# The causal mask of attention, added on VectorE together with the row minimum instead of as products on TensorE

## Chip, cores and metric

The kernel runs on one core of a Trainium2 chip. The metric is the device time of one execution in microseconds, the median of several runs. TensorE multiplies matrices into PSUM; VectorE and ScalarE read PSUM and SBUF and write SBUF here; GpSimd and SyncE mostly start transfers.

## The reference

Two decoder layers over 512 tokens of 1024 channels, in float32: a feed-forward part, a mixer, a second feed-forward part, each followed by a layer norm. The change lies in the mixer's attention. All of its units have this form (shortened):

```
def one_block(args):
    qs, qn, qp = args
    s = (jnp.einsum('bqhd,bkhd->bhqk', qn, k_nope, ...)
         + jnp.einsum('bqhd,bkd->bhqk', qp, k_pe, ...)) * scale
    s = jnp.where(kpos[None, :] <= qpos[:, None], s, NEG)     # causal mask
    p = jax.nn.softmax(s, axis=-1)
    return jnp.einsum('bhqk,bkhd->bqhd', p, v)
```

A layer has 8 heads of latent attention (MLA), and 8 heads of sparse attention (NSA) with two such branches each, over selected blocks and over a window; at this length both branches see all keys up to the query, and so have the same causal mask. A third branch works on 31 compressed keys with a mask of its own (`cmask`).

## The kernel before

Every float32 product is made of two or three products of a high and a low part (`float32r`). Weights come in chunks of 128 rows by up to 1024 columns, in the order of their use: SyncE loads `raw` (ring of 3), ScalarE copies the high part and VectorE subtracts to get the low part (`Stream.pump`, lines 272 and 201, ring `hl` of 4).

A mixer has 24 units of attention a layer: units 0 to 7 are MLA's, with three score passes (`kTh` with `qTh`, `kTl` with `qTh`, `kTh` with `qTl`, 96 rows), 8 to 23 are NSA's, with two passes of 128 rows that hold both parts. A unit (class `Unit`) has four steps. `scores` computes the scores of the four query blocks of 128 (`qb`), each against keys 0 to `(qb + 1) * 128`, so with 128, 256, 384 and 512 columns, into three PSUM banks `sc0` to `sc2`. After a block's passes, line 487 adds one more product into its last 128 columns: identity (`idb`) times mask (`maskb`, 0 or -1e30, both bf16). Line 492 takes the negated row maximum on VectorE (`nm`), and line 493 writes `P = exp(s + nm)` on ScalarE, with the row sum. `normalise` multiplies `P` by the reciprocal of the sum on VectorE (line 503). `transpose` transposes `P` on TensorE into three banks `pt` (line 511), which ScalarE copies to `ph` (line 517) and VectorE subtracts to `pl` (line 201). `pv` multiplies `ph` and `pl` with the values (lines 526 and 527), with the same column counts as the scores: 512, 384, 256, 128.

The order of these steps, and of projections and gate tiles (`gf`) between them, is written out by hand in `SCHEDULE` (S scores, N normalisation, T transposes, P product with values). Within it a scheduler sets each engine's queue; queues run in order. PSUM has eight banks, `P`, `ph` and `pl` come from 55 slabs of 512 columns.

Of the kernel before, what the change touches and what calls it, by code (L numbers as in the profile page):

```python
# [9 lines left out]
F32 = mybir.dt.float32  # L10
F32R = mybir.dt.float32r
BF16 = mybir.dt.bfloat16
AF = mybir.ActivationFunctionType
ALU = mybir.AluOpType
# [3 lines left out]
T = 512  # L18
# [8 lines left out]
NEG = -1e30  # L27

# columns of w_in in the order the kernel projects them
# [7 lines left out]
NSLAB = 55                # [128, 512] tiles for everything that lives for a while  # L37
RAW_RING = 3              # chunks of weights as loaded
HI_RING = 4               # chunks of weights in two parts
LOOK = 2                  # chunks split ahead of their use  # L40
LOOK_TAIL = 5             # the same for the chunks of a tail
LOOK_HEAD = 4             # and right after one
PIECE, PIECES = 256, 1    # the first chunks come in pieces of so many columns
PEND_AT = 3               # head tile before which the pending token blocks are transposed
TAIL = {NF: 5, KB: 4}     # last chunks of a down projection, used token block by token block
PASS, STAY, TAIL_KIND = 0, 1, 2

# The order in which the mixer's attention and what runs beside it is issued. Units of attention 0..23
# (8 heads of MLA, then 2 groups x 4 heads x 2 branches of NSA): Q queries, S scores, N normalisation,
# T transposed probabilities, P product with the values; K keys and G output of a pair of heads. "v" value  # L50
# projections, "m"/"n" halves of gate tiles, "pl"/"p" projection of MLA; "ql".."w" operands of a group,
# "c" compression.
# [62 lines left out]
def layer_plan(l):  # L115
    """Chunks of weights of one layer in the order of their use, each with whether it passes through the
    rings or stays in slabs; a chunk is a list of (matrix, layer, row block, first column, last column)."""
    p = []

    def add(c, kind=PASS):  # L120
        p.append((c, kind))

    def down(name, nkb):
        n = nkb // 2
        for dh in range(2):
            for i in range(n):
                add(down_chunk(name, l, dh, i), TAIL_KIND if dh == 1 and i >= n - TAIL[nkb] else PASS)

    def ffn(n):
        for fi in range(NF):  # L130
            add(stat_chunk(n + "_wg", l, fi * 128))
            add(stat_chunk(n + "_wu", l, fi * 128))
        down(n + "_wd", NF)

    def tok(c0, c1):
        for c in tok_chunks(l, c0, c1):
            add(c)

    ffn("ffn1")
    for m in range(4):  # L140
        add(gate_chunk(l, "m", m))
    tok(COL_A, COL_B)
    tok(COL_B, COL_C)
    add(uq_chunk(l, 0))
    add(uq_chunk(l, 1))
    add(ukv_chunk(l, 0), STAY)
    add(ukv_chunk(l, 1))
    for n in SCHEDULE:
        if n == "keys":
            tok(COL_C, COL_D)  # L150
        elif n == "v0":
            tok(COL_D, COL_GM)
        elif n[0] in "mn" and n[-1] == "a":
            add(gate_chunk(l, n[0], int(n[1])))
        elif n[:2] == "cw":
            add(w1_chunk(l, int(n[2]), int(n[3])))
        elif n == "c2":
            add(w2_chunk(l))
        elif n[0] == "p" and n[1] in "0246":
            add(proj_chunk(l, "w_proj_mla", int(n[1])))  # L160
    for m in range(0, KB, 2):
        add(proj_chunk(l, "w_proj_nsa", m))
    down("w_out", KB)
    ffn("ffn2")
    return p
# [11 lines left out]
def hybrid_kernel(ctx: ExitStack, tc: tile.TileContext, x, wflat, lnp, rmsg, small, cst, out):  # L177
# [40 lines left out]
    class Stream:  # L218
        """Weights in the order of their use: loaded ahead, then split into two float32r parts."""
# [72 lines left out]
    ct = const.tile([128, NCST - 128], F32, name="ct")  # L292

    def cs(name):
        o, n = CST[name]
        return ct[:, o - 128:o - 128 + n]
# [5 lines left out]
    maskb = const.tile([128, 128], BF16, name="maskb")  # L302
# [25 lines left out]
    def head_tiles(chunks, name):  # L328
        """The first weight tiles of a stage, on the tokens in the order in which they come."""
        chs = [W.get(c) for c in chunks]  # L330
        bs = [bank(f"{name}{i}") for i in range(len(chs))]
        for i, (b, ch) in enumerate(zip(bs, chs)):
            if i >= PEND_AT:
                while pend:
                    pend.pop(0)()
            stat_mms(b, ch, 0, 256, range(KB), True, True)
        for b, ch in zip(bs, chs):
            stat_mms(b, ch, 256, 512, range(KB), True, True)
            W.done()
        return bs  # L340

# [28 lines left out]
    def down(lhs, nkb, wname, l, c, eps, ln_idx, last):  # L370
        """xt <- LN(c * x + lhs^T @ w) for every token block; then x^T for the next stage."""
# [94 lines left out]
    class Unit:  # L466
        """One softmax: passes yields (lhsT, rhs) pairs of [K, T] tiles; v(kb) gives the values' two parts
        side by side, so that one product takes both: their shares come out in the two halves of the rows."""
# [6 lines left out]
        def scores(self):  # L475
            ps = [bank(f"sc{i}") for i in range(3)]
            self.P = [slab(f"P{i}") for i in range(3)]
            pp = self.passes()
            self.nm = work.tile([128, TB], F32, tag="nm", bufs=4, name="nm")
            self.l = work.tile([128, TB], F32, tag="l", bufs=4, name="l")  # L480
            for b, qbs in enumerate(BANKS):
                for qb in qbs:
                    off = SC[qb][1]
                    n = (qb + 1) * 128
                    for i, (a, k) in enumerate(pp):
                        mm(ps[b][:, off:off + n], a[:, qb * 128:(qb + 1) * 128], k[:, 0:n], start=i == 0, stop=False)  # L486
                    mm(ps[b][:, off + n - 128:off + n], idb, maskb, start=False, stop=True)  # L487
                for qb in qbs:
                    off = SC[qb][1]
                    n = (qb + 1) * 128  # L490
                    o = ps[b][:, off:off + n]
                    nc.vector.tensor_reduce(out=self.nm[:, qb:qb + 1], in_=o, axis=AX.X, op=ALU.max, negate=True)  # L492
                    act(out=self.P[b][:, off:off + n], in_=o, func=AF.Exp, bias=self.nm[:, qb:qb + 1], scale=1.0,  # L493
                        accum_out=self.l[:, qb:qb + 1])
# [37 lines left out]
    def mixer(l):  # L532
# [42 lines left out]
        # latents of the queries and of the keys and values, with the shared rotary key  # L575
# [24 lines left out]
        def latents():  # L600
# [8 lines left out]
            # below the keys of a head goes the shared rotary key  # L609
# [9 lines left out]
        # NSA queries  # L619
        bb = tok_all(COL_B, COL_C, "pb", latents)  # L620
        for tb in range(TB):
            t = slab(f"nq{tb}")
            act(out=t, in_=bb[tb], func=AF.Copy, scale=0.125)
# [4 lines left out]
        # MLA queries, keys and values  # L628
        scale = float(np.float32(96 ** -0.5))
# [30 lines left out]
        # NSA keys  # L660
# [13 lines left out]
        def halves(b, oc, odd):  # L674
            """Of a head's output the share of the values' high parts, and that of the low parts."""
# [24 lines left out]
        def proj_mla(m):  # L700
            """MLA's share of the gated sum, kept in place of its gates."""
# [20 lines left out]
        def mla_keys(j):  # L722
            """Keys of a pair of heads, in place of those of the pair before."""
# [51 lines left out]
        # gate tiles, in halves  # L775
# [19 lines left out]
        # NSA values and gates  # L795
# [25 lines left out]
        # compressed keys and values  # L821
# [19 lines left out]
        def c_blk(kind):  # L841
            """Rows (token parity, channel), columns (token pair of a window, group, window); the last column
            of a group holds the position embedding, so that the first layer gives its share there."""
# [29 lines left out]
        def c_w1(kind, jh):  # L873
            """Rows: windows, with the blocks' high parts, then with their low ones; columns: the same of the weights."""
# [24 lines left out]
        def c_gelu():  # L899
# [6 lines left out]
            # hidden units of the keys, and those of the values once per head of a group  # L906
# [39 lines left out]
        def group(g):  # L946
# [72 lines left out]
            def c_scores():  # L1019
# [14 lines left out]
                nc.vector.tensor_reduce(out=nm, in_=bv, axis=AX.X, op=ALU.max)  # L1034
                tt(out=pv, in0=bv, in1=nm.to_broadcast([128, 16, 32]), op=ALU.subtract)
                act(out=p, in_=p, func=AF.Exp)
# [71 lines left out]
        # gated sum of the two projections, transposed  # L1108
# [36 lines left out]
    with tc.manual_schedule(engines={mybir.EngineType.Pool}):  # L1145
# [22 lines left out]
        nc.vector.tensor_copy(out=maskb, in_=cs("mask"))  # L1168
# [8 lines left out]
def _constants():  # L1177
# [8 lines left out]
    put("mask", np.where(i[None, :] <= i[:, None], 0.0, NEG))  # L1186
    t = (np.arange(TB)[None, :] * 128 + i[:, None])
    cc = np.arange(32)
    put("cmask", np.where((16 * cc + 31)[None, None, :] <= np.maximum(t, 31)[:, :, None], 0.0, NEG))
# [13 lines left out]
    put("qcc", a * 96 ** -0.5)  # L1203
    put("qss", b * 96 ** -0.5)
# [55 lines left out]
```

## Time and profile before

| | |
|---|---|
| Median of 3 runs | 2288.7 us (2287.52 to 2290.64) |
| Span of the profiled execution | 2289.8 us |
| TensorE busy, of the span | 2274.2 us, 99% |
| VectorE busy | 1181.3 us, 52% |
| ScalarE busy | 859.7 us, 38% |
| Products of line 487 (mask) | 192 |
| Reductions of line 492, Exps of line 493 | 192 each |

The trace is of one execution; it gives a span and no time of its own beside it. TensorE's durations run from a product's start to its modelled end, and products overlap, so the time that a product takes of the engine is read from one start to the next. The attention of layer 1 lies at 468 to 708 us, that of layer 2 at 1602 to 1844 us.

### The profile page before, as it was taken

The page shows a single profiled execution, that of the slowest core. Times are in us where ns is not written, and L with a number is a line of the kernel's source. Part 1 is how long each engine was busy: PE and PEld are TensorE (multiplying, and loading weights), DVE is VectorE, ACT ScalarE, POOL GpSimd, SP SyncE. Part 2 cuts the span into 40 slices and gives each one's busy share as a digit, 9 for nine tenths or more (in the row PEclk, how much of TensorE's full clock was granted, in tenths as well). Part 3 has the DMA queues.
Part 4 walks back from the last instruction along what each step waited for, and adds up shares of the span by engine and source line. Part 5 has one row for each costly group of instructions (what it writes and reads, how often), then busy time and mean ns, then how long its engine had stood idle before and what let it go on. Part 6 is the DMA issues. An engine that isn't in the chain of part 4 may idle for free.

```text
span 2289.8 us, 29329 instructions
## 1 busy us (share of the span) xinstructions
PE 2274.2 (99%) x11590; PEld 1937.3 (85%) x11590; DVE 1181.3 (52%) x2039; ACT 859.7 (38%) x1618; POOL 103.0 (4%) x166
## 2 busy tenths in 40 slices
PE   9999999999999999999999999999999999999998
PEld 8888889998888888888898888899888889888886
DVE  4343335568877644443543433445787866343334
ACT  3222222469764232322222222224786642232220
POOL 0000001010001000000000000010100010000000
PEclk9999999999999999999999999999999999999999
DMA  5323333343225232233323233433432262323331
GB/s 170 102 92 101 107 115 109 121 136 124 93 84 191 99 111 94 100 102 105 115 74 101 92 101 106 139 107 107 126 127 88 70 232 81 102 92 101 106 106 65
DMA packets 86329, 251.57 MB, mean 110 GB/s; under 512 B 18224, under 2 KB 21424, under 8 KB 86192
## 3 DMA queue, kind: packets, MB, share of 16 engines
q1 hardware_dynamic: 75568, 215.09, 28.8%
q0 software_dynamic: 10624, 34.61, 4.3%
q8 instruction: 91, 1.49, 0.3%
q14 instruction: 46, 0.38, 0.1%
HBM read 225.55 MB, written 24.12 MB: 109 GB/s over the span
## 4 chain that ended last, share of the span: by engine, by line
PE 98%; ACT 1%; DMA 1%; DVE 0%; SPq 0%; issue 0%; DVEq 0%; ACTq 0%
PE gu L206 13%; PE gu L205 13%; PE gu L204 13%; PE d L206 8%; PE d L204 8%; PE d L205 8%; PE sc L486 3%; PE pt L511 2%; PE gf L204 2%; PE gf L206 2%; PE gf L205 2%; PE ffh L204 1%; PE ffh L206 1%; PE ffh L205 1%; PE on L527 1%; PE xtp L315 1%
## 5 line engine op out<-in xcount | busy, mean ns | idle before, releaser
L272 ACT ACTIVATE hl<-raw 128x1024 fp32r<-128x1024 f32 (+3 forms) x351 | 361.3, 1031 | 729.5 <-issue 341.8
L201 DVE TENSOR_TENSOR hl<-raw,hl 128x1024 fp32r<-128x1024 f32 (+3 forms) x351 | 416.8, 1189 | 397.7 <-ACT hl L272 397.3
L204 PE MATMUL gu<-xTh,hl 128*128 128x512 f32 x1280 | 498.0, 389 | 0.0
L205 PE MATMUL gu<-xTl,hl 128*128 128x512 f32 x1280 | 498.0, 389 | 0.0
L206 PE MATMUL gu<-xTh,hl 128*128 128x512 f32 x1280 | 497.9, 389 | 0.0
L205 PEld LDWEIGHTS gu<-xTl,hl 128*128 128x128 f32 x1280 | 240.3, 188 | 49.8
L206 PEld LDWEIGHTS gu<-xTh,hl 128*128 128x128 f32 x1280 | 240.3, 188 | 49.8
L204 PEld LDWEIGHTS gu<-xTh,hl 128*128 128x128 f32 x1280 | 240.3, 188 | 49.7
L204 PE MATMUL d<-hl,hh 128*128 128x512 f32 x544 | 211.6, 389 | 0.0
L205 PE MATMUL d<-hl,hh 128*128 128x512 f32 x544 | 211.6, 389 | 0.0
L206 PE MATMUL d<-hl,hl 128*128 128x512 f32 x544 | 211.6, 389 | 0.0
L427 DVE SCALAR_TENSOR_TENSOR t<-t,gu 128x512 f32<-128x512 f32 x80 | 55.0, 688 | 247.7 <-ACT t L426 247.7
L428 DVE TENSOR_TENSOR t<-t,gu 128x512 f32<-128x512 f32 x80 | 55.0, 688 | 210.8 <-PE gu L206 210.8
L426 ACT ACTIVATE t<-gu 128x512 f32<-128x512 f32 x80 | 47.9, 599 | 304.3 <-PE gu L206 304.3
L206 PEld LDWEIGHTS d<-hl,hl 128*128 128x128 f32 x544 | 102.1, 188 | 21.2
L205 PEld LDWEIGHTS d<-hl,hh 128*128 128x128 f32 x544 | 102.1, 188 | 21.2
L204 PEld LDWEIGHTS d<-hl,hh 128*128 128x128 f32 x544 | 102.1, 188 | 21.2
L493 ACT ACTIVATE P<-sc,nm 128x384 f32<-128x384 f32 x192 | 99.5, 527 | 40.6 <-DVE nm L492 32.4
L362 POOL TENSOR_TENSOR rs<-rs,ct 128x1 f32<-128x1 f32 x24 | 22.3, 930 | 1562.3 <-DVE rs L361 1562.3
L201 DVE TENSOR_TENSOR pl<-pt,ph 128x512 fp32r<-128x512 f32 x144 | 78.9, 596 | 24.8 <-ACT ph L517 24.6
L492 DVE TENSOR_REDUCE nm<-sc 128x1 f32<-128x384 f32 x192 | 84.3, 486 | 14.0 <-PE sc L487 11.4
L318 ACT ACTIVATE xTh<-xtp 128x512 fp32r<-128x512 f32 x48 | 26.2, 596 | 157.7 <-PE xtp L315 157.7
(310 smaller groups left out, 3951.3 us busy)
## 6 DMA issues: line engine op xcount, KB each, us to landing
raw<-in_wflat_dram SPq DMA_DIRECT2D x343, 512.0 KB, 3.3
gb<-in_lnp_dram SPq DMA_DIRECT2D x24, 256.0 KB, 4.3
raw<-in_wflat_dram SPq DMA_DIRECT2D x12, 384.0 KB, 3.2
sy<-gl POOLq DMA_DIRECT2D x16, 256.0 KB, 2.3
xr<-spill SPq DMA_DIRECT2D x16, 256.0 KB, 6.2
ym<-sy POOLq DMA_DIRECT2D x16, 256.0 KB, 6.4
raw<-in_wflat_dram SPq DMA_DIRECT2D x8, 416.0 KB, 3.9
raw<-in_wflat_dram SPq DMA_DIRECT2D x8, 408.0 KB, 3.6
```

The costliest lines, as they stand in the source:

```text
L201: tt(out=o, in0=src, in1=f(hi), op=ALU.subtract)
L204: mm(o, lh, rh, start=start, stop=False)
L205: mm(o, lh, rl, start=False, stop=False)
L206: mm(o, ll, rh, start=False, stop=stop)
L272: act(out=h, in_=r[:, j:j + e], func=AF.Copy)
L426: act(out=t, in_=g, func=AF.Tanh, scale=0.5)
L427: stt(out=t, in0=t, scalar=1.0, in1=g, op0=ALU.add, op1=ALU.mult)
L428: tt(out=t, in0=t, in1=u, op=ALU.mult)
L486: mm(ps[b][:, off:off + n], a[:, qb * 128:(qb + 1) * 128], k[:, 0:n], start=i == 0, stop=False)
L492: nc.vector.tensor_reduce(out=self.nm[:, qb:qb + 1], in_=o, axis=AX.X, op=ALU.max, negate=True)
L493: act(out=self.P[b][:, off:off + n], in_=o, func=AF.Exp, bias=self.nm[:, qb:qb + 1], scale=1.0, accum_out=self.l[:, qb:qb + 1])
L511: nc.tensor.transpose(ps[b][:, off + (qb - kb) * 128:off + (qb - kb + 1) * 128], self.P[sb][:, so + kb * 128:so + (kb + 1) * 128], ident)
```

## The change

The mask products go. One instruction of VectorE (`tensor_tensor_reduce`) adds the mask to the scores of a query block, writes the sum to `P` in SBUF, and gives the row minimum; Exp then works in place on `P` with scale -1. For the minimum to serve, the queries are negated (by the scale that they get anyway, and by the rotary tables `qcc` and `qss`), and the mask is 0 or +1e30. The mask is now float32, 512 columns wide (`maskw`: zeros in front, the triangle in the last 128 columns), so that one operand serves every block. The compressed branch takes a minimum in place of a maximum too; its mask stays a product.

```diff
-    maskb = const.tile([128, 128], BF16, name="maskb")
+    maskw = const.tile([128, T], F32, name="maskw")
...
                     for i, (a, k) in enumerate(pp):
-                        mm(ps[b][:, off:off + n], a[:, qb * 128:(qb + 1) * 128], k[:, 0:n], start=i == 0, stop=False)
-                    mm(ps[b][:, off + n - 128:off + n], idb, maskb, start=False, stop=True)
+                        mm(ps[b][:, off:off + n], a[:, qb * 128:(qb + 1) * 128], k[:, 0:n], start=i == 0,
+                           stop=i == len(pp) - 1)
...
-                    o = ps[b][:, off:off + n]
-                    nc.vector.tensor_reduce(out=self.nm[:, qb:qb + 1], in_=o, axis=AX.X, op=ALU.max, negate=True)
-                    act(out=self.P[b][:, off:off + n], in_=o, func=AF.Exp, bias=self.nm[:, qb:qb + 1], scale=1.0,
+                    o = self.P[b][:, off:off + n]
+                    nc.vector.tensor_tensor_reduce(out=o, in0=ps[b][:, off:off + n], in1=maskw[:, T - n:T], scale=1.0,
+                                                   scalar=BIG, op0=ALU.add, op1=ALU.min, accum_out=self.nm[:, qb:qb + 1])
+                    act(out=o, in_=o, func=AF.Exp, bias=self.nm[:, qb:qb + 1], scale=-1.0,
                         accum_out=self.l[:, qb:qb + 1])
...
-            act(out=t, in_=bb[tb], func=AF.Copy, scale=0.125)
+            act(out=t, in_=bb[tb], func=AF.Copy, scale=-0.125)
...
-        nc.vector.tensor_copy(out=maskb, in_=cs("mask"))
+        nc.vector.memset(maskw[:, 0:T - 128], 0.0)
+        nc.vector.tensor_copy(out=maskw[:, T - 128:T], in_=cs("mask"))
```

TensorE's queue at the scores of unit 21 in layer 1 (`sc` are its banks, `ks` the keys, `qs` the queries), before:

```order
L486 MATMUL sc_6240<-ks_5567,qs_5372 128x384
L486 MATMUL sc_6240<-ks_5430,qs_5372 128x384
L487 LDWEIGHTS idb
L487 MATMUL sc_6240<-maskb,idb 128x128
L486 MATMUL sc_6240<-ks_5567,qs_5372 128x128
L486 MATMUL sc_6240<-ks_5430,qs_5372 128x128
L487 LDWEIGHTS idb
L487 MATMUL sc_6240<-maskb,idb 128x128
L486 MATMUL sc_6241<-ks_5567,qs_5372 128x512
L486 MATMUL sc_6241<-ks_5430,qs_5372 128x512
```

The same place now:

```order
L486 MATMUL sc_6157<-ks_5504,qs_5321 128x384
L486 MATMUL sc_6157<-ks_5375,qs_5321 128x384
L486 MATMUL sc_6157<-ks_5504,qs_5321 128x128
L486 MATMUL sc_6157<-ks_5375,qs_5321 128x128
L486 MATMUL sc_6158<-ks_5504,qs_5321 128x512
L486 MATMUL sc_6158<-ks_5375,qs_5321 128x512
```

The mask products and their weight loads are gone, and the score products stand in the same order. Elsewhere TensorE's queue is the same but for one exchange in each layer: three products of a gate tile and the two 384-column products of a unit with its values.

VectorE's queue at that place, where the low parts `pl` of units 18 and 19 and the reductions of unit 21 meet, before:

```order
L201 TENSOR_TENSOR pl_6206<-pt_6190,ph_6203 128x512
L201 TENSOR_TENSOR pl_6207<-pt_6191,ph_6204 128x512
L201 TENSOR_TENSOR pl_6208<-pt_6192,ph_6205 128x256
L492 TENSOR_REDUCE nm<-sc_6240 128x1
L201 TENSOR_TENSOR pl_6231<-pt_6215,ph_6228 128x512
L201 TENSOR_TENSOR pl_6232<-pt_6216,ph_6229 128x512
L201 TENSOR_TENSOR pl_6233<-pt_6217,ph_6230 128x256
L492 TENSOR_REDUCE nm<-sc_6241 128x1
L492 TENSOR_REDUCE nm<-sc_6240 128x1
L492 TENSOR_REDUCE nm<-sc_6242 128x1
L497 RECIPROCAL l<-l 128x4
```

And now:

```order
L201 TENSOR_TENSOR pl_6148<-pt_6132,ph_6145 128x512
L201 TENSOR_TENSOR pl_6149<-pt_6133,ph_6146 128x512
L201 TENSOR_TENSOR pl_6150<-pt_6134,ph_6147 128x256
L492 ISA P_6160,nm<-sc_6157,maskw 128x384
L492 ISA nm 128x1
L492 ISA P_6160,nm<-sc_6157,maskw 128x128
L492 ISA nm 128x1
L492 ISA P_6161,nm<-sc_6158,maskw 128x512
L492 ISA nm 128x1
L492 ISA P_6162,nm<-sc_6159,maskw 128x256
L492 ISA nm 128x1
L498 RECIPROCAL l<-l 128x4
```

Each reduction has become two rows, of which the second writes the accumulator to `nm`; a unit's four stand together, behind the low parts of both units, and the two blocks in bank `sc0` now come first. ScalarE's Exps follow the same order.

## Rows read from the trace of the kernel before

**Rows 1.** The page: busy time, share of the span and instructions of each engine; and the chain that ended last, by engine.

```profile
PE 2274.2 (99%) x11590; PEld 1937.3 (85%) x11590; DVE 1181.3 (52%) x2039; ACT 859.7 (38%) x1618; POOL 103.0 (4%) x166
...
PE 98%; ACT 1%; DMA 1%; DVE 0%; SPq 0%; issue 0%; DVEq 0%; ACTq 0%
```

**Rows 2.** What TensorE waited for in the mixers, from the view of its waits over the whole span: us in total, times, longest.

```profile
PE cd L854 <- DMA lc<-sv: 0.5, 2, 0.2
PE om L685 <- ACT oe L678: 0.5, 2, 0.2
PE om L526 <- DVE pl L201: 0.4, 2, 0.2
```

**Rows 3.** Busy time by stretch, the attention of both layers: stretch, its length, busy us of each engine (and instructions), granted share of TensorE's clock, share of the DMA engines, GB/s.

```profile
468.00:690.00 222.00, 221.37 (x1371) 190.93 (x1370) 174.41 (x413) 165.47 (x432) 19.03 (x32) 0.99 0.33 106
1602.00:1825.00 223.00, 222.37 (x1369) 192.03 (x1368) 173.82 (x411) 164.75 (x430) 18.82 (x32) 0.98 0.33 105
```

**Rows 4.** TensorE in order of time at the scores of an NSA unit: start, us, instruction.

```profile
622.82 0.51 PE L486 MATMUL sc<-ks,qs 128*128 128x384 f32 x2
623.17 0.23 PE L487 MATMUL sc<-maskb,idb 128*128 128x128 bf16 x1
623.21 0.42 PE L486 MATMUL sc<-ks,qs 128*128 128x128 f32 x2
623.47 0.23 PE L487 MATMUL sc<-maskb,idb 128*128 128x128 bf16 x1
...
624.42 0.23 PE L487 MATMUL sc<-maskb,idb 128*128 128x128 bf16 x1
624.46 0.52 PE L997 MATMUL ksT<-idr,kdh 128*128 128x128 f32 x4
```

**Rows 5.** The same view at a unit's product with the values; the first of each pair of equal width, and what follows the last pair.

```profile
633.08 0.39 PE L526 MATMUL on<-ph,nv 128*128 128x512 f32 x1
...
633.53 0.33 PE L526 MATMUL on<-ph,nv 128*128 128x384 f32 x1
...
633.88 0.28 PE L526 MATMUL on<-ph,nv 128*128 128x256 f32 x1
...
634.12 0.23 PE L526 MATMUL on<-ph,nv 128*128 128x128 f32 x1
...
634.29 0.51 PE L997 MATMUL ksT<-idr,kdh 128*128 128x128 f32 x4
```

**Rows 6.** The same view at the scores of the compressed branch, 32 columns each, and what follows them.

```profile
598.43 0.26 PE L1026 MATMUL cs<-kch,qs 128*128 128x32 f32 x1
598.54 0.26 PE L1027 MATMUL cs<-kcl,qs 128*128 128x32 f32 x1
598.65 0.26 PE L1026 MATMUL cs<-kch,qs 128*128 128x32 f32 x1
...
599.25 1.78 PE L511 MATMUL pt<-ident,P 128*128 128x128 f32 x10
```

**Rows 7.** The same view at another product with the values, right behind the last mask product of unit 21's scores: the mask product, the first of the eight, and what follows them.

```profile
681.53 0.23 PE L487 MATMUL sc<-maskb,idb 128*128 128x128 bf16 x1
681.57 0.47 PE L526 MATMUL on<-ph,nv 128*128 128x512 f32 x1
...
682.87 1.28 PE L511 MATMUL pt<-ident,P 128*128 128x128 f32 x10
```

**Rows 8.** The same view at the scores of an MLA unit: the first of twelve products, and what follows the last mask.

```profile
508.17 0.39 PE L486 MATMUL sc<-kTh,qTh 96*128 96x384 f32 x1
...
510.53 0.28 PE L511 MATMUL pt<-ident,P 128*128 128x128 f32 x1
```

**Rows 9.** Groups of instructions by line, shapes kept apart: operation, shapes, count, busy us, mean ns of one, idle time before. VectorE's and, last, ScalarE's read-out of its accumulator.

```profile
L201 DVE TENSOR_TENSOR pl<-pt,ph 128x512 fp32r<-128x512 f32 x96 | 62.4, 685 | 23.6 <-ACT ph L517 23.4
...
L492 DVE TENSOR_REDUCE nm<-sc 128x1 f32<-128x512 f32 x48 | 33.0, 687 | 2.4 <-PE sc L487 2.0
...
L368 DVE SCALAR_TENSOR_TENSOR xr<-xr,rs,gb 128x512 f32<-128x512 f32 x40 | 28.2, 747 | 0.0
...
L492 DVE TENSOR_REDUCE nm<-sc 128x1 f32<-128x128 f32 x48 | 13.7, 285 | 1.6 <-ACT P L493 1.6
...
L361 DVE TENSOR_SCALAR rs<-mv 128x1 f32<-128x1 f32 x24 | 3.7, 154 | 0.8
...
L493 ACT ACTIVATION_READ_ACCUMULATOR P<-sc,nm 128x1 f32 x192 | 38.6, 201 | 0.0
```

**Rows 10.** The same view: two copies on ScalarE, the first reads PSUM, the second SBUF.

```profile
L517 ACT ACTIVATE ph<-pt 128x512 fp32r<-128x512 f32 x96 | 52.9, 599 | 14.1 <-PE pt L511 14.1
...
L689 ACT ACTIVATE oh<-oc 128x512 fp32r<-128x512 f32 x16 | 10.2, 637 | 7.7 <-DVE oc L688 7.6
```

**Rows 11.** VectorE in order of time at the second place of the order above: start, us, instruction, idle time before it.

```profile
679.70 1.62 DVE L201 TENSOR_TENSOR pl<-pt,ph 128x512 fp32r<-128x512 f32 x3 [0.53 <-ACT ph L517]
681.24 0.55 DVE L492 TENSOR_REDUCE nm<-sc 128x1 f32<-128x384 f32 x1
681.70 1.61 DVE L201 TENSOR_TENSOR pl<-pt,ph 128x512 fp32r<-128x512 f32 x3
...
685.61 0.18 DVE L497 RECIPROCAL l<-l 128x4 f32<-128x4 f32 x1 [1.17 <-ACT P L493]
```

**Rows 12.** The same view, VectorE's first instruction of the program.

```profile
2.76 0.23 DVE L1164 CAST idb<-ident 128x128 bf16<-128x128 f32 x1 [2.76 <-DMA ident<-in_cst_dram]
```

**Rows 13.** Busy time by stretch as in rows 3, two microseconds in the first layer's attention; the granted clock is the third figure from the end.

```profile
600.00:602.00 2.00, 2.00 (x8) 1.81 (x7) 2.00 (x6) 1.57 (x4) 0.00 (x0) 0.50 0.03 8
```

More of the change, by code (lines that the diff above doesn't have):

```diff
@@ L26 @@
 RMS_EPS = 1e-6
-NEG = -1e30
+BIG = 1e30
 COL_A = 0
@@ L626, in mixer @@
             nc.gpsimd.dma_start(out=sp_q[:, tb, :], in_=t)
-        scale = float(np.float32(96 ** -0.5))
+        scale = -float(np.float32(96 ** -0.5))
         mq, VP, vt = {}, {}, {}
@@ L1033, in c_scores @@
                 pv = p.rearrange("p (a c) -> p a c", c=32)
-                nc.vector.tensor_reduce(out=nm, in_=bv, axis=AX.X, op=ALU.max)
+                nc.vector.tensor_reduce(out=nm, in_=bv, axis=AX.X, op=ALU.min)
                 tt(out=pv, in0=bv, in1=nm.to_broadcast([128, 16, 32]), op=ALU.subtract)
-                act(out=p, in_=p, func=AF.Exp)
+                act(out=p, in_=p, func=AF.Exp, scale=-1.0)
                 nc.vector.tensor_reduce(out=cl, in_=pv, axis=AX.X, op=ALU.add)
@@ L1185, in _constants @@
     put("ident", np.eye(128))
-    put("mask", np.where(i[None, :] <= i[:, None], 0.0, NEG))
+    put("mask", np.where(i[None, :] <= i[:, None], 0.0, BIG))
     t = (np.arange(TB)[None, :] * 128 + i[:, None])
     cc = np.arange(32)
-    put("cmask", np.where((16 * cc + 31)[None, None, :] <= np.maximum(t, 31)[:, :, None], 0.0, NEG))
+    put("cmask", np.where((16 * cc + 31)[None, None, :] <= np.maximum(t, 31)[:, :, None], 0.0, BIG))
     put("blk", np.repeat((((i // 32) % 2)[:, None] == np.arange(2)[None, :]).astype(np.float32), 64, axis=1))
@@ L1202, in _constants @@
     put("kss", b)
-    put("qcc", a * 96 ** -0.5)
-    put("qss", b * 96 ** -0.5)
+    put("qcc", a * -96 ** -0.5)
+    put("qss", b * -96 ** -0.5)
     a, b = tables(16)
```

## The prediction

> **What bounds the kernel now.** I read the page's busy shares and its chain first. TensorE is busy for 2274.2 of 2289.8 us and holds 98% of the chain [rows 1]. A busy TensorE can still hide waits, so the second view is what TensorE waited for over the span. In the mixers there are six waits, 1.4 us in all [rows 2]. Nothing but TensorE's own sequence of products sets the end, also in the two stretches where the masks are. So a product that goes gives its time back in full, as long as no other engine moves into the gap.
>
> The third view is the two attention stretches. In 222 us of the first, VectorE is busy for 174.41 us (79%) and ScalarE for 165.47 (75%); the second layer reads the same [rows 3]. VectorE has 47.6 us to spare there, while it is idle for half of the span as a whole. This stretch, and not the span, decides about the change.
>
> **What goes: 192 mask products on TensorE.** The group's own row would say 231 ns each, but these durations overlap. What counts is from start to start. A sparse unit's scores run from 622.82 to 624.46, 1.64 us for eight products and four masks [rows 4]. The mask's own slot is short: one starts at 623.17 and the next score product at 623.21, 0.04 us. The rest of its price shows in its neighbours: the 128-column pair behind it lasts from 623.21 to 623.47, 0.26 us [rows 4].
>
> For the price without masks I need eight products of the same shapes in a row. A unit's product with the values is that: pairs of 512, 384, 256 and 128 columns, 0.45, 0.35, 0.24 and 0.17 us, 1.21 us together [rows 5]. That gives 1.64 - 1.21 = 0.43 us a unit. Two corrections: the short pair stands in the middle of the scores, where a following weight load can't hide behind it. Products of 32 columns, which hide nothing, are 0.11 us apart [rows 6], so I charge the pair 0.22 in place of 0.17, and the gain falls to 0.38. Against that, the last mask also delays what follows the unit: the same eight products right behind a mask last from 681.57 to 682.87, 1.30 us in place of 1.21 [rows 7], so up to 0.09 us more comes back, less where transposes follow. Bounds 0.38 and 0.52; I take 0.43, since half of the tail makes up for the short pair.
>
> A unit of the first eight has three passes: 2.36 us from 508.17 to 510.53 [rows 8]. Without masks, one and a half times 1.26 is 1.89 us, so I take 0.47. A layer has 16 and 8 units: 16 x 0.43 + 8 x 0.47 = 10.6 us, and **21.3 us for both layers**. With the bounds of 0.38 and 0.52 for all 48 units it is 18 to 25.
>
> **What comes: VectorE.** Four reductions a unit become four masked adds with a minimum. The built program has a second instruction behind each, which writes the accumulator out: eight rows a unit in place of four.
> - The main instruction reads PSUM and SBUF, writes SBUF, and reduces. No row shows all of this at once. The reduction alone takes 687 ns at 512 columns; a subtraction that reads PSUM and SBUF and writes SBUF takes 685 [rows 9]. Upper bound: the two-operation form with two SBUF inputs and a pointer scalar, 747 [rows 9]. I take no difference, since reading and writing beside each other cost nothing in the nearest row. Bounds 0 and 0.06 us.
> - The read-out is in no row of VectorE. The nearest there is an instruction with one column, 154 ns; ScalarE's read-out of its accumulator takes 201 [rows 9]. I take 154, an estimate; an unseen handover could make it cheaper, not below zero.
>
> [...]
>
> So a unit gets 4 x 0.154 = 0.62 us more of VectorE, 24 units 14.8. The stretch then has 189.2 us of VectorE in 222 - 10.6 = 211.4 us, 89%. At the upper bounds, 4 x (0.06 + 0.20) = 1.04 us a unit, it is 199.4, 94%. Both still lie beside TensorE on the sum.
>
> **The wait that it adds.** Exp now reads P in SBUF, which VectorE has just written, and waits for the read-out of the minimum. That is 0.15 us later for each Exp; behind it in ScalarE's queue stand the copies of the transposed probabilities and the weights' high parts. Reading SBUF costs ScalarE a little more: a 512-column copy takes 637 ns from SBUF and 599 from PSUM [rows 10]. 96 times 38 ns is 3.6 us a layer, 169.1 of 211.4 us, 80%: covered. The score banks come free after VectorE's instruction and no longer after Exp; but no wait of TensorE in the mixers names a score bank [rows 2], so that gives nothing.
>
> **What VectorE's lateness costs.** The sum of busy time fits; the order may not. In the place that the order shows, the low parts pl of one unit take from 679.70 to about 681.3, and the product that reads them starts at 681.57 [rows 7, 11]. TensorE will ask some 0.4 us earlier. VectorE then has its reductions for the new unit, and in the changed order both units' pl stand ahead of them, which helps here. After that it is idle again, waiting 1.17 us for ScalarE at 685.61 [rows 11]: such gaps end the lateness before it adds up. So I charge 0.25 us at five places of a layer, **2.5 us** in all, a judgement; its ends are nothing and the first rival's 12.6.
>
> **Edits with no price.** The wider mask table is cleared by VectorE at the start, 384 columns, while VectorE waits 2.76 us for the identity [rows 12]. If that cover were gone it would cost one instruction of half a microsecond. Signs of queries, tables and Exp are constants in instructions that stay. Two products of the values change places with three of a gate tile in each layer; nothing waits there.
>
> **The sum.** The trace has one execution with a span of 2289.8 us; the runs gave 2287.5 to 2290.6, median 2288.7, so nothing to speak of lies around the span. 2288.7 - 21.3 + 2.5 = 2269.9, forecast **2270 us**. [...]
>
> **Rivals.**
> - **VectorE comes late and TensorE waits for it.** For it: 89 to 94% busy, and margins such as 0.25 us [rows 7, 11]. One place can lose what VectorE was charged since it last stood still, one unit's 0.62, plus the 0.43 by which TensorE asks earlier: 1.05 us. If a quarter of a layer's 24 units lose it whole, that is 6.3 us a layer, 12.6 in all: 2288.7 - 21.3 + 12.6 = **2280**. Against it: the gaps in VectorE's row.
> - **Slower: the new instruction streams at half rate.** Two tensors are read, one written, and the accumulator is fed. The slope of the reduction is (687 - 285) / 384 = 1.05 ns a column [rows 9]; a second one for 1280 columns is 1.34 us a unit, 32.2 a layer. VectorE would need 174.4 + 14.8 + 32.2 = 221.4 us in the stretch, with no idle time at all, and its chain through ScalarE leaves some. With a fifth of today's 47.6 us, 9.5, the stretch lasts 230.9 in place of 222: +8.9 us a layer, **2306**. VectorE is the bound from (211.4 - 174.4) / 24 = 1.5 us more a unit, and the kernel slower than before from 47.6 / 24 = 2.0, which is 0.5 us more for each reduction. Against it: neither the subtraction from PSUM nor the form with two SBUF inputs is slower than 747 ns [rows 9]. [...]
> - **The gaps stay.** If the spacing around a mask were the score products' own, only its slot of 0.04 us would go: 192 x 0.04 = 7.7, less 2.5, **2283.5**. The 1.30 against 1.21 us of the same products [rows 5, 7] speaks against it.
>
> **How the numbers follow.** What a measurement of this kernel can tell from no change is about 0.2%, 4.6 us: 2284.1 to 2293.3. Forecast, 2264 to 2275: 0.62. Late VectorE, 2275 to 2284: 0.16, and in its worse tail no change: 0.05. Gaps stay: 0.05, of which 0.02 in the zone of no change. Half rate or another heavy price on VectorE: 0.12, of which 0.02 would come out as no change and 0.10 slower. So faster 0.81, the same 0.09, slower 0.10. The low end takes the upper bound of the masks' price and no lateness, 2288.7 - 25 = 2264; the high end takes in the first rival, 2284, and leaves out the slower cases.
>
> **What would show it.** Score groups of a sparse unit at 1.21 to 1.28 us from first to next. [...] VectorE at 85 to 94% of an attention stretch of about 211 us. New waits of TensorE on pl, P or nm of 1 to 6 us in all. The forecast is wrong if the new instruction takes over 1.1 us at 512 columns, if waits of TensorE on VectorE exceed 6 us, or if the score groups stay above 1.4 us.

## The result, and the profile after

The changed kernel takes **2275.6 us** (median of four runs, 2270.1 to 2278.3); the kernel before took 2289.6 beside it (2287.5 to 2290.6). The ratio is **0.9936, 95% interval 0.9924 to 0.9948**: 14 us faster, where 19 were forecast. The time lies in the predicted range. The profiled execution has a span of 2276.5 us, 13.3 less than that of before.

TensorE's scores first, in order of time: start, us, instruction. An NSA unit (its eight products are one row, the next row is what follows):

```profile
583.93 1.44 PE L486 MATMUL sc<-ks,qs 128*128 128x384 f32 x8
585.21 0.40 PE L527 MATMUL on<-ph,nv 128*128 128x512 f32 x1
```

It takes 1.28 us in place of 1.64 [rows 4]. An MLA unit goes from 506.46 to 508.44, 1.98 us in place of 2.36 [rows 8]:

```profile
506.46 0.39 PE L486 MATMUL sc<-kTh,qTh 96*128 96x384 f32 x1
...
508.44 1.26 PE L512 MATMUL pt<-ident,P 128*128 128x128 f32 x10
```

VectorE in order of time, the four blocks of a unit:

```profile
586.23 0.55 DVE L492 CUSTOM_DVE_ANT_0 P<-sc,maskw 128x384 f32<-128x384 f32 x1
586.71 0.08 DVE L492 DVE_READ_ACCUMULATOR2_ANT nm<- 128x1 f32 x1
586.71 0.28 DVE L492 CUSTOM_DVE_ANT_0 P<-sc,maskw 128x128 f32<-128x128 f32 x1
586.92 0.08 DVE L492 DVE_READ_ACCUMULATOR2_ANT nm<- 128x1 f32 x1
586.92 0.69 DVE L492 CUSTOM_DVE_ANT_0 P<-sc,maskw 128x512 f32<-128x512 f32 x1
587.53 0.08 DVE L492 DVE_READ_ACCUMULATOR2_ANT nm<- 128x1 f32 x1
```

The read-out starts in the same instant as the next main instruction. The first row has 384 columns, and the next block starts 0.48 us behind it; before, what followed the 384-column reduction started 0.46 behind it [rows 11]. So a block costs VectorE 0.02 us more, and not the length of the read-out. The main instruction itself, groups of instructions as in rows 9:

```profile
L492 DVE CUSTOM_DVE_ANT_0 P<-sc,maskw 128x512 f32<-128x512 f32 x48 | 32.9, 686 | 0.0
...
L492 DVE DVE_READ_ACCUMULATOR2_ANT nm<- 128x1 f32 x192 | 16.0, 83 | 0.0
```

686 ns at 512 columns; the reduction took 687 [rows 9]. The page's first row, and the two attention stretches with the columns of rows 3, say what that makes of VectorE:

```profile
PE 2258.4 (99%) x11398; PEld 1940.4 (85%) x11398; DVE 1180.7 (52%) x2232; ACT 863.0 (38%) x1618; POOL 102.6 (5%) x166
```

```profile
468.00:680.00 212.00, 210.57 (x1259) 189.64 (x1258) 169.66 (x490) 164.44 (x425) 18.30 (x31) 0.98 0.34 111
1590.00:1803.00 213.00, 210.57 (x1254) 190.11 (x1253) 165.95 (x477) 161.06 (x414) 18.30 (x31) 0.98 0.35 110
```

VectorE does 1180.7 us, as it did before (1181.3 [rows 1]), and stands at 80 and 78% of the stretches, not at 89.

What TensorE waited for, over the span (the first and the last row lie outside the mixers and are as before):

```profile
PE xtp L315 <- DMA x<-in_x_dram: 4.6, 2, 4.3
PE cd L855 <- DMA lc<-sv: 3.6, 2, 2.3
PE ffh L204 <- ACT hl L272: 1.0, 1, 1.0
```

It waits for no result of VectorE or ScalarE in the mixers any more; both waits of that kind in rows 2 are gone. But the wait for `lc`, the reload of the values that are to be compressed, has grown from 0.5 to 3.6 us.

The last difference is the clock. The stretches of the mixers at half the granted clock (the third figure from the end), the changed kernel first and then the kernel before, with the columns of rows 3:

```profile
593.00:599.80 6.80, 6.80 (x30) 6.24 (x30) 5.79 (x10) 3.55 (x7) 0.00 (x0) 0.51 0.09 23
640.80:644.20 3.40, 3.40 (x15) 3.20 (x16) 2.82 (x5) 1.97 (x4) 0.00 (x0) 0.52 0.47 154
1722.80:1726.20 3.40, 3.40 (x18) 3.21 (x18) 3.40 (x7) 2.45 (x5) 0.00 (x0) 0.53 0.01 2
1767.20:1774.00 6.80, 6.80 (x27) 6.15 (x27) 4.68 (x10) 1.99 (x4) 0.00 (x0) 0.51 0.32 111
```

```profile
599.70:603.10 3.40, 3.40 (x14) 2.92 (x13) 3.40 (x8) 1.98 (x4) 0.00 (x0) 0.53 0.02 5
1733.00:1736.40 3.40, 3.40 (x18) 3.30 (x18) 3.40 (x9) 2.20 (x4) 0.00 (x0) 0.52 0.00 0
1780.80:1784.20 3.40, 3.40 (x13) 2.83 (x11) 3.30 (x9) 1.87 (x4) 0.00 (x0) 0.51 0.18 72
```

20.4 us at a granted clock of 0.51 to 0.53 in place of 10.2 (inside each stretch it stands at 0.50). TensorE is busy in all of them; each begins in or behind one of the four groups of narrow products (`cs`, 32 columns) and the transposes beside it. The price is read at the end of the first one, TensorE in order of time:

```profile
598.53 0.63 PE L204 MATMUL pm<-oh,hl 128*128 128x512 f32 x1
598.96 0.63 PE L205 MATMUL pm<-ol,hl 128*128 128x512 f32 x1
...
600.37 0.40 PE L206 MATMUL pm<-oh,hl 128*128 128x512 f32 x1
600.60 0.39 PE L204 MATMUL pm<-oh,hl 128*128 128x512 f32 x1
```

Products of 512 columns start 0.43 us apart, and behind it 0.23. By that spacing some 46% of such a stretch is lost: 1.6 us of each 3.4, an estimate.

**The account of the two profiles.** From the first product of each group of scores to the start of the third product behind the group, summed over all groups, the kernel before takes 106.9 us and the changed one 86.7: **20.2 less** (18.3 of it within the groups). The wait for `lc` gives back 3.1, the waits on `pl` and `oe` bring 0.9, and 10.2 us more at half clock cost about 4.7. That is 20.2 - 3.1 + 0.9 - 4.7 = 13.3, the difference of the spans. The 4.7 is an estimate, 46% of 10.2, and the profiled execution is the slowest of the changed kernel's four runs (2278.3 us); the fastest had the highest clock (0.997).

### The profile page after: what moved, and what is told of

It is laid out like the page before. It is cut to its first block, busy times and chain, and to the rows that moved or that the text cites. A ratio compares the mean times of both kernels' runs of the same rounds, so it can differ in the third digit from the quotient of the medians.

```text
span 2276.5 us, 29167 instructions
## 1 busy us (share of the span) xinstructions
PE 2258.4 (99%) x11398; PEld 1940.4 (85%) x11398; DVE 1180.7 (52%) x2232; ACT 863.0 (38%) x1618; POOL 102.6 (5%) x166
## 4 chain that ended last, share of the span: by engine, by line
PE 97%; ACT 1%; DMA 1%; DVE 1%; issue 0%; SPq 0%; DVEq 0%; ACTq 0%
PE gu L205 13%; PE gu L204 13%; PE gu L206 13%; PE d L204 8%; PE d L206 8%; PE d L205 8%; PE sc L486 3%; PE pt L512 2%; PE gf L204 2%; PE gf L206 1%; PE gf L205 1%; PE ffh L204 1%; PE ffh L206 1%; PE ffh L205 1%; PE on L528 1%; PE xtp L315 1%
## 5 line engine op out<-in xcount | busy, mean ns | idle before, releaser
L494 ACT ACTIVATE P<-P,nm 128x384 f32<-128x384 f32 x192 | 105.5, 552 | 39.5 <-DVE nm L492 35.6
L492 DVE CUSTOM_DVE_ANT_0 P<-sc,maskw 128x384 f32<-128x384 f32 x192 | 82.8, 485 | 7.1 <-PE sc L486 7.0
```

The lines of the kernel that those rows point to most:

```text
L492: nc.vector.tensor_tensor_reduce(out=o, in0=ps[b][:, off:off + n], in1=maskw[:, T - n:T], scale=1.0, scalar=BIG, op0=ALU.add, op1=ALU.min, ...
L494: act(out=o, in_=o, func=AF.Exp, bias=self.nm[:, qb:qb + 1], scale=-1.0, accum_out=self.l[:, qb:qb + 1])
```

## The experiments

**Theory.** TensorE gains 20 us, VectorE's new work costs nothing, and what is missing went to the clock and to the reload. **Rival:** VectorE comes late somewhere, and the waits named are only where that shows. Each ratio is to the kernel before, measured beside the run. The clock is the mean granted clock over each run's span, lowest and highest of the runs.

| run | median, us | range | ratio to before, 95% interval | clock |
|---|---|---|---|---|
| changed kernel | 2275.6 | 2270.1 to 2278.3 | 0.9936 (0.9924 to 0.9948) | 0.995 to 0.997 |
| no_mask_old_vector | 2273.1 | 2266.6 to 2275.7 | 0.9921 (0.9907 to 0.9934) | 0.995 to 0.999 |
| new_vector_kept_masks | 2290.7 | 2287.3 to 2292.7 | 1.0000 (0.9991 to 1.0009) | 0.996 to 0.998 |
| mask_twice | 2303.1 | 2301.2 to 2303.5 | 1.0056 (1.0042 to 1.0070) | 0.996 |
| vector_plus_one | 2275.3 | 2272.0 to 2278.9 | 0.9934 (0.9919 to 0.9949) | 0.994 to 0.997 |
| vector_twice | 2320.1 | 2318.1 to 2321.9 | 1.0132 (1.0118 to 1.0145) | 0.989 to 0.991 |
| cb1_later | 2273.5 | 2273.0 to 2274.6 | 0.9927 (0.9915 to 0.9940) | 0.995 to 0.996 |
| cs_split | 2272.6 | 2271.8 to 2273.4 | 0.9922 (0.9910 to 0.9935) | 0.999 |
| both_repairs | 2274.7 | 2274.1 to 2275.8 | 0.9934 (0.9921 to 0.9946) | 0.998 to 0.999 |
| before_split | 2288.6 | 2287.1 to 2289.6 | 0.9992 (0.9983 to 1.0001) | 0.998 to 0.999 |
| after_split | 2271.2 | 2269.8 to 2271.4 | 0.9915 (0.9902 to 0.9929) | 0.999 |
| after_split_cb1 | 2270.7 | 2269.7 to 2271.7 | 0.9914 (0.9901 to 0.9928) | 0.999 |
| after_split_t14 | 2269.3 | 2268.9 to 2271.2 | 0.9913 (0.9899 to 0.9926) | 0.999 |

### TensorE's part alone

```
-   mm(ps[b][:, off:off + n], a[...], k[:, 0:n], start=i == 0, stop=False)
-mm(ps[b][:, off + n - 128:off + n], idb, maskb, start=False, stop=True)
+   mm(ps[b][:, off:off + n], a[...], k[:, 0:n], start=i == 0, stop=i == len(pp) - 1)
```

> The kernel before without the 192 mask products, nothing put in their place (so its output has no causal mask); VectorE and ScalarE as before. Theory (the scores' spacing gave about 20 us on TensorE, VectorE's new work costs nothing, and what is missing was lost to TensorE's granted clock and to a wait for the compressed values' reload): as the changed kernel, 2268 to 2278 us, sparse score groups 1.27 us apart, the wait cd<-lc 2 to 4 us. Rival (VectorE comes late somewhere in the changed kernel): 2 to 5 us faster than the changed kernel, 2265 to 2272.

2273.1, in the theory's range and 1 us above the rival's; the interval overlaps the changed kernel's, so this alone doesn't separate them. The wait for `lc`, which the theory put at 2 to 4 us, is 1.0 here, since the build placed three more products of a gate tile ahead of the transposes that read it; so this run takes away a part of that wait along with VectorE's work. Its runs at a clock of 0.995 and 0.996 have 2271.5 to 2275.7, the one at 0.999 has 2266.6: most of the spread goes with the clock.

### VectorE's part alone

```
+mm(ps[b][:, off + n - 128:off + n], idb, maskw[:, 0:64].bitcast(BF16), start=False, stop=True)
 nc.vector.tensor_tensor_reduce(out=o, in0=ps[b][:, off:off + n], ...
```

> The changed kernel with a mask product kept on TensorE in every place, of zeros: VectorE's part alone. Theory: VectorE's part is free, so the time is that of the kernel before, 2286 to 2292 us, score groups of 1.64 us and no wait of TensorE on VectorE. Rival (VectorE's work costs): 2293 or more, with waits on P, nm or pl.

The kernel before, within the 2 us of the interval: VectorE's part is free. One thing was not expected, a wait for `lc` of this size with the masks still there:

```profile
PE cd L856 <- DMA lc<-sv: 2.4, 2, 1.6
```

So the wait doesn't come from TensorE's gain alone. Part of it comes from an exchange in TensorE's queue, whose order the build sets: this kernel and the changed one have it, the kernel before and `no_mask_old_vector` don't. (Its waits are 1.0 us more in all than those of the kernel before, since the waits on `pl` and `oe` of rows 2 are gone here too; the medians can't show so little.) The kernel before at this place, in order of time:

```profile
514.40 0.60 PE L746 MATMUL qT<-ident,mq 128*96 128x128 f32 x4
514.76 0.48 PE L204 MATMUL gf<-xTh,hl 128*128 128x512 f32 x1
515.08 0.39 PE L205 MATMUL gf<-xTl,hl 128*128 128x512 f32 x1
515.31 0.40 PE L206 MATMUL gf<-xTh,hl 128*128 128x512 f32 x1
515.95 0.63 PE L854 MATMUL cd<-ident,lc 128*128 128x128 f32 x4 [0.25 <-DMA lc<-sv]
```

And the changed kernel:

```profile
512.30 0.60 PE L747 MATMUL qT<-ident,mq 128*96 128x128 f32 x4
514.22 0.63 PE L855 MATMUL cd<-ident,lc 128*128 128x128 f32 x4 [1.32 <-DMA lc<-sv]
```

Three products of a gate tile stood ahead of the transposes `cd` and gave the reload some 0.7 us in each layer. Now they stand behind. Another 0.4 a layer is TensorE's gain on the scores of the unit between (2.36 to 1.98 us): the reload's chain (the last product of step `v3`, ScalarE's copy, a write to memory, a read back) moves up only as far as `v3` does. The last 1.0 us is the chain itself: from the last product of `v3` to `cd` it takes 10.0 to 10.1 us in both layers of the kernel before and in the first one here, but 11.0 in the second one here. Why stays open; where `cd` waits for it in the other profiles, it takes 9.8 to 11.1.

### What a mask product costs

```
 mm(ps[b][:, off + n - 128:off + n], idb, maskb, start=False, stop=False)
+mm(ps[b][:, off + n - 128:off + n], idb, maskb, start=False, stop=True)
```

> The kernel before with every mask product issued twice in a row (192 more products; the masked places get the mask added twice, the output is the same). If the mask's price of 0.107 us lies in each product, 20 us more than the kernel before: 2308 to 2313. If it lies in the change from the score products to one short product and back, and a second product beside it costs only its own slot of 0.04 to 0.055 us, 7 to 11 us more: 2297 to 2302.

12.9 us more, a time between the two cases. The trace decides between them. An NSA unit's scores, TensorE in order of time, the first products and what follows the last mask:

```profile
624.42 0.51 PE L486 MATMUL sc<-ks,qs 128*128 128x384 f32 x2
...
626.29 0.52 PE L998 MATMUL ksT<-idr,kdh 128*128 128x128 f32 x4
```

1.87 us in place of 1.64 for four more masks, 0.057 each. Counted as in the account above, all groups take 117.8 us in place of 106.9, 0.056 for each added product, so the second case holds. The other 2 us lie outside the groups; this profile has 13.6 us of the mixers at half clock in place of 10.2, at 1.6 for each 3.4 most of it. The first mask of a group costs 20.2 / 192 = 0.105 us, one more behind it 0.056. So about 0.05 of the price is the change between wide and short products, paid once, and the rest goes with each product. The rival "the gaps stay", with 0.04 for each, is refuted by the 0.105.

### How much VectorE could bear

```
+for _ in range(2 if qb == 3 else 1):        # vector_plus_one; vector_twice: for every block
     nc.vector.tensor_tensor_reduce(out=o, in0=ps[b][:, off:off + n], ...
```

> The changed kernel with the masked minimum of the 512-column block issued twice (0.77 us of VectorE more a unit, 18.5 a layer; VectorE some 88% of an attention stretch, which is what the prediction thought the changed kernel would have). Theory (VectorE has room, and its lateness does not reach TensorE): 2274 to 2279 us, under 1.5 us of TensorE's waits on VectorE and ScalarE in the mixers. Rival (at such a load its lateness costs what the prediction's first rival charges, 1.05 us at a quarter of the units): 2281 to 2289, with waits of 6 to 12 us on pl, P or sc.

> The changed kernel with all four masked minima of a unit issued twice (2.27 us of VectorE more a unit, 54.5 a layer, where an attention stretch has some 42 idle): 168 + 54.5 = 222.5 us of VectorE in a stretch of 211. Both theories see VectorE as the bound here. If it can use all of its time, the stretch lasts 223 to 226 us and the kernel 2300 to 2307; if a fifth of today's idle time can't be used, some 231, and 2315 to 2320.

With one more instruction a unit, VectorE stands at 86 and 83% of the stretches, near the load that the prediction gave the changed kernel:

```profile
468.00:680.00 212.00, 209.84 (x1262) 188.76 (x1261) 182.49 (x536) 166.35 (x428) 19.02 (x31) 0.98 0.35 110
1590.00:1803.00 213.00, 210.46 (x1255) 190.03 (x1253) 177.55 (x520) 163.17 (x417) 18.95 (x31) 0.98 0.35 111
```

The time is that of the changed kernel, and the only new wait in the mixers is 1.1 us on `qs` from ScalarE. The rival on VectorE's lateness (2281 to 2289) is refuted at this load. With four more TensorE waits for VectorE, 30.8 us in all by the waits that name it, and the time is at the upper end of the expectation's upper case, 2320.1. VectorE isn't full even so: the same stretches have it at 86 and 84%, no more than with one more instruction, so its share alone doesn't tell whether TensorE waits. Their granted clock is 0.95 and 0.96 in place of 0.98; how much of the 44.5 us is the clock's no run separates. The longest of these waits:

```profile
PE qsT L971 <- DVE qst L201: 9.1, 2, 4.5
PE pt L514 <- DVE P L506: 6.1, 2, 3.1
```

### The reload and the clock

```
-Q5 cb1 G0 N4 P2 T3 cx0          +Q5 G0 N4 P2 T3 cb1 cx0           (cb1_later)
-T10 cs0 N11 qt10 T11 p1 pl4 n2a +T10 cs0a p1 cs0b N11 n2a qt10 T11 pl4   (cs_split)
-cs1 T14 n4b                     +cs1a n4b cs1b T14                (cs_split)
```

`cs0a` issues the narrow products of the first two token blocks, `cs0b` those of the other two and the softmax; `cs1` likewise.

> The changed kernel with one step moved in the order: the transposes of the reloaded compressed values (cb1) go behind three other steps (G0, P2, T3), about 3 us later. Theory: the wait cd<-lc falls from 3.6 us to under 0.5 and the time by 2 to 3.5 us against the changed kernel, as far as the clock's falls don't blur it. Rival (the wait only stands in front of another that is as late): the wait goes, and another of like size comes, the time stays within 1 us.

The wait for `lc` went, and two others came:

```profile
PE om L527 <- ACT ph L518: 1.9, 2, 0.9
...
PE om L528 <- DVE pl L201: 0.4, 2, 0.2
```

2.3 us of waits in place of 3.6, and a median 2.1 us lower, as the theory had it; but all its runs lie within the range of the changed kernel's, so the time alone doesn't show a gain. The waits are more as the rival had them.

> The changed kernel with the 32 narrow products of the compressed scores (cs, twice a layer) issued in two halves, with a projection step or half a gate tile (12 products of 512 columns) between, and other dense steps before the transposes behind. The same work. Theory (the narrow products and the transposes beside them are what precedes each stretch of granted clock 0.50, and those 20.5 us cost some 8 to 10 us): fewer and shorter stretches at 0.50, under 10 us in all, and 4 to 8 us less than the changed kernel. Rival (the falls come whatever stands there, or cost nothing): 15 to 25 us at 0.50 as before, time within 2 us of the changed kernel.

All falls of the clock in the mixers are gone. The attention of both layers, columns as in rows 3:

```profile
468.00:700.00 232.00, 229.07 (x1385) 204.37 (x1384) 186.33 (x540) 178.13 (x461) 19.91 (x34) 1.00 0.35 112
1590.00:1830.00 240.00, 236.66 (x1422) 210.76 (x1421) 187.18 (x541) 180.89 (x465) 19.94 (x35) 1.00 0.35 113
```

So the narrow products in one block are what the falls follow. The median falls by 3.0 us only, less than the theory's 4 to 8 and more than the rival's 2. New waits, 1.9 us more in all, stand beside the old one:

```profile
PE cd L855 <- DMA lc<-sv: 3.2, 2, 1.8
PE gf L204 <- DVE nm L492: 1.4, 2, 0.7
...
PE ct L1053 <- DVE pc L1046: 0.6, 2, 0.3
```

### Both repairs

```
-Q5 cb1 G0 N4 P2 T3 cx0 S5 pl1 m4b N5  +Q5 m4b cb1 G0 N4 P2 T3 cx0 S5 pl1 N5
-T10 cs0 N11 qt10 T11 p1 pl4 n2a       +T10 cs0a p1 cs0b N11 qt10 T11 pl4 n2a
-ct0 qt12 P11 qt11                     +qt12 P11 ct0 qt11
-cs1 T14 n4b                           +cs1a n4b cs1b T14
```

> The changed kernel with two moves in the order: half a gate tile (m4b, 12 products) ahead of the reloaded values' transposes (cb1), and a projection step or half a gate tile between the two halves of the narrow products (cs), with the transposes of the compressed probabilities (ct0) one step later. The same work. Theory: no wait cd<-lc, no stretch at granted clock 0.50 in the mixers, and no new wait over 0.5 us: 2289.6 - 21 - 5 (the falls that the kernel before had as well) + 1 = 2263 to 2268 us. Rival (a repair makes another wait of like size each time): 2270 to 2274.

The rival, clearly, and 0.7 us above its range: no fall (mean clock 0.999 in the profiled run), no wait for `lc`, and 8.1 us of new waits.

```profile
PE qsT L969 <- DVE qst L201: 3.8, 2, 1.9
PE om L686 <- ACT oe L679: 2.6, 2, 1.3
PE gf L204 <- DVE nm L492: 1.4, 2, 0.7
```

The likely reason is that the half gate tile is missing where it used to stand, so that TensorE meets operands behind it that aren't ready; no run shows this by itself.

### The change at an equal clock

Both kernels with the same split: `p1` between the halves of `cs0`, `n4b` between those of `cs1`, `ct0` behind `P11`, `n5a` behind `P14`. `after_split_cb1` also has `Q5 G0 N4 T3 P2 cb1 cx0`, and `after_split_t14` has `cs1a n4b T14 cs1b` in place of `cs1a n4b cs1b T14`.

> The kernel before, with masks on TensorE and the old VectorE form, and the narrow products cs in two halves with 12 wide products between; ct0 stands one step later, and half a gate tile (n5a) one step later. The same work. Theory (the falls of the granted clock follow the narrow products, and each of 3.4 us costs some 1.6 us): no stretch at 0.50 in the mixers, and 4 to 5.5 us less than the kernel before: 2284 to 2287 us. Rival (the falls are harmless, TensorE being limited by something else there): within 1.5 us of the kernel before.

> The changed kernel with exactly the same moves as in before_split. Theory: no stretch at 0.50 in the mixers, no wait gf<-nm, the wait cd<-lc of 3 to 3.6 us stays: 2269 to 2271.5 us, and 15 to 17 us less than before_split, the masks' 20 less the wait for the reload. Rival (what is missing of the 21 us lies in VectorE's new work, not in clock and reload): the difference stays at 12 to 14 us, with waits on P, nm or pl.

> after_split, with the reloaded values' transposes cb1 behind G0, T3 and P2, and T3 ahead of P2. Theory: the wait cd<-lc goes and the high parts ph are there when P2 asks, so under 0.7 us of new waits, 2266 to 2268.5 us, 18 to 20 us less than before_split. Rival (P2 then waits for ph as in cb1_later, 1.9 us): 2268.5 to 2270.5.

> after_split, with the transposes of unit 14 (T14) ahead of the second half of the narrow products of the second group (cs1), so that ScalarE copies ph of unit 14 before the softmax of cs1. Theory (the wait on<-ph of 1.6 us stood behind that softmax in ScalarE's and VectorE's queues): the wait goes, no stretch at 0.50 in the mixers, 1 to 1.6 us less than after_split: 2269.5 to 2270.5. Rival (TensorE has nothing else to do there and takes the wait at the next step): as after_split, 2271 to 2272.

`before_split` has no fall in the mixers and gains 1.5 us only, short of the theory's 4 to 5.5 and at the edge of the rival's, since the waits there are 3.5 us in place of 1.4; most is this one, which the kernel before doesn't have:

```profile
PE sc L486 <- ACT P L493: 2.5, 2, 1.3
```

So the clock gave back 3.6 us, 1.2 a stretch, against the 1.6 that the rows gave; what the split itself costs isn't separated. `after_split`:

```profile
PE cd L855 <- DMA lc<-sv: 3.2, 2, 2.2
PE on L527 <- ACT ph L518: 1.6, 2, 0.8
```

It is 17.3 us faster than `before_split` where both run at the full clock, above the theory's 15 to 17 and well above the rival's 12 to 14. Its waits in the mixers are 5.1 us, 1.6 more; 17.3 + 1.6 = 18.9, and the groups of scores give 20.1 here (110.6 to 90.5 us, counted as above). 0.4 of that is waits that lie within the groups (2.5 and 2.1 us); the other 0.8 I can't place.

`after_split_cb1` has no wait for `lc`, but 4.7 us of others, and the time of `after_split`: both the theory's time and its list of waits were wrong, and its time is 0.2 us above the rival's range.

```profile
PE pt L512 <- DVE pl L201: 1.6, 2, 0.8
PE sc L486 <- DVE pl L201: 1.2, 4, 0.4
```

`after_split_t14` is the fastest kernel here, **2269.3, ratio 0.9913**. But the wait that it was to remove is still there under another name:

```profile
PE on L527 <- DVE nm L492: 1.8, 2, 0.9
```

So the mechanism that I wrote down is refuted though the time came out within 0.2 us of what was written. Its median is 1.9 us lower, and the lowest run of `after_split` lies within its range; in the profiles 0.9 us of the difference arise ahead of the first mixer: the first products with weights start 0.21 us apart up to 12.8 us of the span of `after_split`, and 0.12 apart from 10.9 us on here. What the move itself is worth stays open.

## Why the prediction was right, and where it was not

- **What bounds the kernel: right.** VectorE's part alone gives 2290.7 against 2290.8 us, TensorE's part alone 2273.1. Products taken from TensorE come back as time. ScalarE's slower reads were covered, as predicted: its Exp of 512 columns takes 710 ns from SBUF where it took 689 from PSUM, and it stands at 78 and 76% of the stretches.
- **The masks' price: right, a little high.** 21.3 predicted, 20.2 measured, bounds 18 to 25. The units came out at 1.28 and 1.98 us in place of 1.21 and 1.89. The correction for the short pair in the middle of the scores, 1.26 in an NSA unit, was the nearer one (in the trace of before the weight loads of the 32-column products start 0.11 us apart, as the products do, and are busy for 2.00 of the 2.00 us from 596 to 598), and the tail gives 1.9 us in all. The rival "the gaps stay" is refuted.
- **VectorE's term: mis-sized.** The prediction added 154 ns a block, 14.8 us a layer. The read-out has a record of 83 ns but lies beside the next instruction; from start to start a block costs 0.02 us more, some 2 us a layer. The trace has 192 read-outs for 192 blocks.
- **"What VectorE's lateness costs", 2.5 us: wrong, it is nothing.** No wait of TensorE in the mixers names VectorE, and at 86% (vector_plus_one) there is still none. The rival of 2280 is refuted up to that load; the 89 to 94% that it assumed were not run. Its mechanism is real with four more instructions a unit, 2320, and in the runs that change the order, where waits of up to 3.8 us name VectorE.
- **Half rate: refuted.** 686 ns at 512 columns, with one source in PSUM and one in SBUF, where the reduction took 687 [rows 9]; no run here has this instruction with both sources in SBUF.
- **"Nothing waits there": the step that failed.** Under the edits with no price, the prediction let three products of a gate tile and two of the values change places. It read them against each other, and not against what they both passed: the transposes `cd`, where the only wait for a DMA in the mixers stood [rows 2]. Moved behind them, they no longer cover the reload. 3.1 us more wait in all, against a charge of nothing: some 1.4 from the exchange, 0.75 from TensorE's own gain on the scores ahead of `cd`, 1.0 from a slower reload in the second layer, whose cause stays open.
- **The clock: no term in the sum.** A stretch of 3.4 us costs 1.6 us by the spacing of the products and 1.2 by before_split, both estimates. Rows 13 lie in one such stretch; the mixers of that trace have three. In the changed kernel 10.2 us more stand at half clock, some 4.7 us of time, in the profiled run. That narrow products in one block precede the falls is shown by cs_split and before_split. Why there are more and longer ones in the changed kernel is not. vector_twice aside, where TensorE waits, the unsplit profiles without masks have 13.7 to 20.5 us of the mixers at half clock and those with masks 10.2 to 13.6; their runs have clocks of 0.994 to 0.999 and of 0.996 to 0.998, and no run varied that alone.

So the forecast of 2270 misses by 5.6 us, by the account of the profiles: 1.1 on the masks, 3.1 on the reload, 4.7 on the clock, less 2.5 charged to VectorE and 0.9 of old waits that went. The mechanism of the gain was right; that the miss is no larger is in part luck, since the 2.5 us for a lateness that didn't come stand against 7.8 that were charged with nothing.

## What to carry to other kernels

When work leaves the engine that sets the end, list what this engine waits for today, however little, and look there first: what it gains it spends at the next operand, and a product that changes places is costed against what it passes. A wait that is repaired by order alone can come back at another operand: each of the moves here left 2 to 8 us of waits in place of 3.6. And compare kernels at an equal granted clock, or their difference holds the clock's share too.

## What the runs showed of the hardware

- A read-out of VectorE's accumulator is recorded with 83 ns and starts with the next main instruction (both at 586.71 us); a block costs 0.02 us more from start to start (0.48 against 0.46 at 384 columns).
- In the mixers of before and of the changed kernel TensorE's granted clock fell to 0.50, for 3.4 or 6.8 us at a time, while it was busy without a gap, at narrow products 0.11 us apart [rows 6] and transposes or behind them. With twelve products of 512 columns between the halves of them it reads 1.00 around them in cs_split, before_split and after_split_t14; the profiled runs of all six kernels with that split have a mean clock of 0.999, and every run of them 0.998 or 0.999.
- A 128-column bf16 product behind wide ones costs 0.105 us (20.2 us for 192), and a second one behind it 0.056 (10.9 us for 192).
